# Five loads of each preparation, and the stores behind the scan, issued from GpSimd's queue instead of SyncE's

## The chip, the cores and the metric

The kernel runs on one core of one Trainium2 chip. The metric is the device time of one execution in microseconds, as the median of several runs. TensorE does the matrix products, VectorE (DVE in the profile) and ScalarE (ACT) the elementwise work. SyncE (SP) and GpSimd (POOL) issue the DMAs; GpSimd also runs a few memsets. Each engine works through its own instructions in order, so an instruction that waits holds back whatever stands behind it on that engine, DMA issues included.

## The reference

Two groups of 512 tokens with 1024 channels go through the same two layers. Layer 0 is a bidirectional RWKV-7 mixer with 16 heads of 64 channels, layer 1 a windowed attention on an 8 x 64 grid. What matters here:

```
r, k, v = lerp(0) @ w_r, lerp(1) @ w_k, lerp(2) @ w_v ;  z = xn @ w_z
kk = k * k_k ;  kk = kk / max(sqrt(sum(kk * kk)), 1e-12)          # per head
for d in range(2):                                                # forward and backward
    decay = exp(-exp(w_log(w0[d] + tanh(xw @ w1[d]) @ w2[d])))
    a     = sigmoid(a0[d] + (xa @ a1[d]) @ a2[d])
    k_d   = k * (1 + (a - 1) * k_a)
    y    += scan: S_t = S_{t-1} (diag(decay_t) - kk_t (kk_t a_t)^T) + v_t k_d_t^T ;  y_t = S_t r_t
x = x + rms(out(y) * silu(z)) ;  q, k, v, z = rms(x) @ w_in + b_in
o = softmax(q k^T / 8 + bias, in a window) v ;  y = x + rms((o * silu(z)) @ w_ao + b_ao)
```

All arithmetic is float32. A large product is done as three passes on values split into a high and a low part.

## The kernel before

A tile is 128 partitions by 512 columns of float32, 256 KB. The work has three parts.

**The part before the scan** loads the two inputs, normalizes them and makes z and k of the first group. Its stores go through SyncE, because the attribute `away` is False.

**The scan** (`scan_phase`) is woven from threads. The scan is done in 64 steps: eight chunks of 64 tokens, for each of two groups and four pairs of channel groups. Beside it run the large products of the layer: r and v of group 0, then k, r, v and z of group 1, then the first output projection and part of the second layer's input projection. Their weights come in through `raw` buffers (three of them), are split into `whi` and `wlo`, and multiplied at lines 811 to 813; their operands come in through `xr`.

Before the steps of a pair can run, two preparations (`prep`, one per channel group of 128 channels, 16 in all) have to be done. A preparation begins with five loads: the reciprocal norms `rb` in two halves, `k`, the low-rank factors `w2`, and `r`. Its first arithmetic is line 863 on DVE, which needs `k` and `rb`; line 865 on ACT and line 867 on DVE split `w2`; the products with `r` come later, at line 925. The tiles `rb`, `k` and `r` have one buffer each, so that the next preparation's loads wait until the one before has read them: `rb` until line 928 of its second direction, `k` until line 940, `r` until line 976. The tile for `w2` is one of the five `tmp` buffers. A preparation makes, for each direction, a 1 MB tile `ab` that goes to DRAM (line 944), from where the steps fetch it (`cab`), and at the end the tile `ks` (line 976), which is saved as well.

**The part behind the scan** (`rest`) finishes the input projections of the second layer, runs the attention heads beside them, and ends with the output projection of the second group. The projections are saved to DRAM (q, k, v, z), and `heads` loads them again.

What sets the order of the work: in the scan the order of TensorE, DVE and ACT is written out by a planner that works while the kernel is built. It keeps a clock per engine and per DMA issuer, and steps the thread of the best rank whose inputs will be there. A DMA on SyncE moves that issuer's clock by 380 ns, a DMA on GpSimd by 900 ns (`Clock.one`); its landing follows from the same formula for both. The order within SyncE's and GpSimd's own queues, and all orders before and behind the scan, are made by the scheduler of the framework, which has a timeline of its own. All orders are fixed before the kernel runs.

DMA issuers: `load` always uses SyncE. `save` asks `store(kind)`, which is GpSimd while `away` is True and the kind is none of y, x1 and h. `scan_phase` sets `away` to True at its start, `rest` to False. Stores on GpSimd's queue in the scan are thus `ab`, `ks`, r, v and its transposed form `vt`, k and z of group 1, and the first q, k, v, z of layer 1. At the start of the scan GpSimd also clears two large `MT` tiles (line 1659), and in every direction of a preparation it sets a pad of the tile `e` (line 902).

Of the kernel before, what the change touches and what calls it, by code (L numbers as in the profile page):

```python
# [19 lines left out]
P = 128  # L20
T = 512
# [210 lines left out]
class Trunk:  # L232
# [96 lines left out]
    def store(self, kind):  # L329
        return self.nc.gpsimd if self.away and kind not in ("y", "x1", "h") else self.nc.sync  # L330

    def load(self, dst, src):
        self.nc.sync.dma_start(dst, src)
        return dst

    def vectors(self):
# [495 lines left out]
    def prep(self, s, p):  # L832

        nc, sp = self.nc, self.sp
        vt, gps, act = nc.vector, nc.gpsimd, nc.scalar
        c3 = lambda t: t.rearrange("p (c t) -> p c t", c=NCH)
        half = lambda h: slice(64 * h, 64 * h + 64)
# [15 lines left out]
                yield "S"  # L853
        k, r, rb = b("k"), b("r"), b("rb")
        for h in range(2):
            self.load(rb[half(h)], sp["rn", s, 0][2 * p + h:2 * p + h + 1, :].to_broadcast([64, T]))
        self.load(k, sp["k", s, p])
        w2l, w2h = b("w2l", (P, 4 * P), 1, F32R), b("w2h", (P, 4 * P), 1, F32R)
        w2 = self.load(self.tmp(), self.a["lora2"][p])
        self.load(r, sp["r", s, p])  # L860
        yield "D", None, need(k, rb)
        kk = rb
        vt.scalar_tensor_tensor(kk, k, self.vec("kk", p), rb, op0=ALU.mult, op1=ALU.mult)
# [10 lines left out]
        for d in range(2):  # L874
            ths = []
            for q, bias in ((d, 8 * d + p), (2 + d, 16 + 8 * d + p)):
                yield "P", free, lambda c: max(room(c), need(w2l, w2h)(c))
                ps = self.p("pm")
                h = self.hid[q]
# [605 lines left out]
    def out1(self, s):  # L1485
        nc = self.nc
        x = self.os[s]
        acc = self.t("acc1", pool=self.ap)
        hs = []
        for p in range(NP):  # L1490
            ps = yield from self.gemm(self.weight(self.a["w_ao"][p]), x, self.OUT1[p % 4])
            h = self.t("oa", (P, T), NP, F32, self.ap)
            nc.scalar.activation(h, ps, AF.Identity, bias=self.vec("bo", p))
            self.sumsq(acc, h, p, nc.vector if p == NP - 1 else nc.vector)
            hs.append(h)
            yield
        yield from self.rstds(acc, lambda: self.mm)
        rstd = acc
        for k, h in enumerate(hs):
            x = self.load(self.t("xr", bufs=self.NXR), self.sp["x1", s, k])  # L1500
            one = nc.vector.scalar_tensor_tensor(h, h, self.vec("post1", k), rstd, op0=ALU.mult, op1=ALU.mult)
            self.behind(one, self.mq)
            (nc.vector if k % 2 else nc.vector).tensor_tensor(h, h, x, op=ALU.add)
            nc.sync.dma_start(self.a["y"][s][k * P:(k + 1) * P, :], h)
            yield

    def by_token(self):
# [211 lines left out]
    def run(self):  # L1719
        self.todo = [(s, pb) for s in range(2) for pb in range(4)]  # L1720
        self.made, self.hid, self.shift = set(), {}, {}
        self.did = Counter()
        self.xz, self.os = [], [[], []]
        self.spare = None
        self.away = False
        mid, prep, first = ExitStack(), ExitStack(), ExitStack()
        self.banks(mid, pf=1, pm=5 - self.SG - self.ZY, us=1)
        if self.SG:
            self.banks(mid, pg=self.SG)
        self.zs = ExitStack()  # L1730
        self.banks(self.zs, zy=self.ZY)
        self.gt = "zy"
        self.lp = self.pool(first, "right")
        a = self.prelude(0)
        for _ in range(self.FIRST):
            next(a)
        a = both(a, self.prelude(1))
        run(self.columns(0, "z", self.xz), (a, 1))
        run(self.columns(0, "k", self.shifted(0, 1)), (a, 1))
        run(a)  # L1740
        self.xr = self.shifted(0, 0)
        first.close()
        self.front = self.pool(mid, "right")
        self.pp = self.pool(prep, "right")
        self.AHEAD, self.AHEADW = self.SCAN_A, self.SCAN_W
        self.scan_phase(mid)
        self.rest(prep, mid)

    def rest(self, prep, mid):
        self.away = False  # L1750
        prep.close()
        mid.close()
        self.banks(self.stack, pg=self.PG, pt=self.PT, po=1, sc=1, pm=5 - self.PG - self.PT)
        self.gt = "pg"
        self.ap = self.pool(self.stack)
        queue = [self.heads(0, p) for p in range(self.NPA)]

        def attention():
            while True:
                if queue and next(queue[0], self) is self:  # L1760
                    queue.pop(0)
                    continue
                yield

        a = attention()
        for p in range(self.NPA, NP):
            run(self.inproj(0, self.xa, p), (a, self.POST0))
            queue.append(self.heads(0, p))
        run(self.out0(1), (a, self.POST))
        while queue:  # L1770
            next(a)
        o = self.out1(0)
        if self.HS:
            with self.tc.high_priority(self.HS):
                next(o)
        n = KT * NP
        for _ in self.norm0(1):
            for _ in range(min(n, 3)):
                next(o)
                n -= 1  # L1780
        for _ in range(n):
            next(o)
        x = self.x1
        xt = self.by_token()
        for p, cs in [(p, range(4)) for p in range(6)] + [(6, range(3)), (7, range(3)), (6, (3,)), (7, (3,))]:
            run(self.inproj(1, x, p, cs), (a, self.POST3), (o, self.POST2), (xt, self.POST4))
            if 0 in cs:
                queue.append(self.heads(1, p))
        run(o)
        while queue:  # L1790
            next(a)
        self.last()
# [125 lines left out]
```

## Time and profile before

| | |
|---|---|
| median of 3 runs | 1663.77 us (1659.5 to 1666.94) |
| the profiled execution: its own time | 1661.37 us |
| its span, first to last instruction | 1659.6 us |
| mean granted TensorE clock in it | 0.979 |
| scan, about | 170 to 1165 us of the span |
| DMAs issued in the scan, SyncE and GpSimd | 678 and 183 |
| DMAs issued behind the scan, SyncE and GpSimd | 312 and 1 |

In a row of a timeline the columns are start, duration, engine, line, operation, tiles, count, and in brackets the idle time of the engine before it and what ended it. "SPq" is SyncE issuing a DMA. In a row of the waits the columns are who waited for what, the time in total, how many times, and the longest. In a table by windows each engine has its busy time and the number of its instructions, then come the granted clock, the busy share of the DMA engines and the rate.

### The profile page before, as it was taken

The page shows a single profiled execution, that of the slowest core. Times are in us where ns is not written, and L with a number is a line of the kernel's source. Part 1 is how long each engine was busy: PE and PEld are TensorE (multiplying, and loading weights), DVE is VectorE, ACT ScalarE, POOL GpSimd, SP SyncE. Part 2 cuts the span into 40 slices and gives each one's busy share as a digit, 9 for nine tenths or more (in the row PEclk, how much of TensorE's full clock was granted, in tenths as well). Part 3 has the DMA queues.
Part 4 walks back from the last instruction along what each step waited for, and adds up shares of the span by engine and source line. Part 5 has one row for each costly group of instructions (what it writes and reads, how often), then busy time and mean ns, then how long its engine had stood idle before and what let it go on. Part 6 is the DMA issues. An engine that isn't in the chain of part 4 may idle for free.

```text
span 1659.6 us, 46414 instructions
## 1 busy us (share of the span) xinstructions
PE 1557.8 (94%) x18826; PEld 1193.4 (72%) x18826; DVE 1226.3 (74%) x2725; ACT 984.7 (59%) x1979; POOL 145.4 (9%) x278
## 2 busy tenths in 40 slices
PE   7989888898989998999988999999999999999998
PEld 5867566776767776776766777777777788777776
DVE  8995669688789787897788897855676585754564
ACT  5443665766756677665575665454677665555562
POOL 0000113311101224010000011000000000000000
PEclk9989999999999999999987999999999999999999
DMA  6435678776676788675867675554864346655553
GB/s 212 160 126 173 206 243 280 221 244 214 228 255 225 222 260 247 219 255 173 253 220 228 196 253 165 182 189 129 289 219 156 102 153 229 214 159 172 165 159 108
DMA packets 179894, 336.27 MB, mean 203 GB/s; under 512 B 20928, under 2 KB 53824, under 8 KB 179680
## 3 DMA queue, kind: packets, MB, share of 16 engines
q1 hardware_dynamic: 160864, 268.28, 50.2%
q0 software_dynamic: 18816, 65.02, 11.9%
q8 instruction: 148, 2.42, 0.6%
q14 instruction: 66, 0.54, 0.1%
HBM read 227.71 MB, written 105.51 MB: 201 GB/s over the span
## 4 chain that ended last, share of the span: by engine, by line
PE 46%; DVE 7%; DMA 6%; ACT 5%; issue 3%; POOL 0%; SPq 0%; DVEq 0%; ACTq 0%; POOLq 0%
PE pg L428 6%; PE pg L429 5%; PE pg L430 5%; PE pm L811 4%; PE pm L812 3%; PE pm L813 3%; PE sc L1437 2%; PE pf L1099 2%; DMA dk<-tmp 2%; PE po L1470 2%; PE us L1218 1%; PE pt L1455 1%; PE zy L1171 1%; PE us L1198 1%; PE zy L1222 1%
## 5 line engine op out<-in xcount | busy, mean ns | idle before, releaser
L811 PE MATMUL pm<-act,whi 128*128 128x512 f32 x640 | 283.6, 443 | 11.9 <-ACT whi L730 5.0
L812 PE MATMUL pm<-act,whi 128*128 128x512 f32 x640 | 257.1, 402 | 10.6 <-DVE act L758 6.5
L813 PE MATMUL pm<-act,wlo 128*128 128x512 f32 x640 | 256.1, 400 | 6.0 <-DVE wlo L732 5.9
L811 PEld LDWEIGHTS pm<-act,whi 128*128 128x128 f32 x640 | 122.0, 191 | 55.3 <-issue 11.4
L377 ACT CAST whi<-raw 128x512 fp32r<-128x512 f32 x148 | 91.5, 618 | 114.0 <-PE pg L429 67.1
L428 PE MATMUL pg<-act,whi 128*128 128x512 f32 x384 | 157.9, 411 | 0.4 <-DVE tmp L1393 0.4
L430 PE MATMUL pg<-act,wlo 128*128 128x512 f32 x384 | 152.1, 396 | 0.0
L429 PE MATMUL pg<-act,whi 128*128 128x512 f32 x384 | 152.0, 396 | 0.0
L812 PEld LDWEIGHTS pm<-act,whi 128*128 128x128 f32 x640 | 122.5, 191 | 36.6 <-DVE act L758 15.8
L813 PEld LDWEIGHTS pm<-act,wlo 128*128 128x128 f32 x640 | 122.4, 191 | 36.2 <-DVE wlo L732 9.6
L378 DVE TENSOR_TENSOR wlo<-raw,whi 128x512 fp32r<-128x512 f32 x148 | 101.5, 687 | 54.6 <-ACT whi L377 52.6
L732 DVE TENSOR_TENSOR wlo<-raw,whi 128x512 fp32r<-128x512 f32 x160 | 109.0, 684 | 35.5 <-ACT whi L730 35.2
L730 ACT CAST whi<-raw 128x512 fp32r<-128x512 f32 x160 | 97.9, 618 | 44.6 <-PE pm L812 23.4
L428 PEld LDWEIGHTS pg<-act,whi 128*128 128x128 f32 x384 | 72.2, 188 | 15.8 <-issue 3.3
L430 PEld LDWEIGHTS pg<-act,wlo 128*128 128x128 f32 x384 | 72.2, 188 | 15.5 <-issue 0.7
L429 PEld LDWEIGHTS pg<-act,whi 128*128 128x128 f32 x384 | 72.4, 189 | 13.2 <-issue 1.5
L1003 DVE TENSOR_TENSOR etmp<-N 128x30 f32<-128x30 f32 (+14 forms) x240 | 78.6, 328 | 4.3
L1005 DVE TENSOR_TENSOR N<-etmp,N 128x30 f32<-128x30 f32 (+14 forms) x240 | 78.7, 328 | 4.0
L1448 DVE CUSTOM_DVE_ANT_0 sb<-sc,bias 128x256 f32<-128x256 f32 x128 | 49.3, 419 | 34.6 <-PE pt L1455 22.7
L1451 ACT ACTIVATE sb<-sb,mx 128x256 f32<-128x256 f32 x128 | 64.0, 503 | 8.6 <-DVE mx L1450 8.1
L1099 PE MATMUL pf<-cab 64*64 64x128 f32 (+1 forms) x2048 | 66.6, 266 | 0.8 <-issue 0.8
L1210 ACT COPY X<-us 64x256 f32<-64x256 f32 x128 | 46.9, 366 | 25.3 <-PE zy L1077 21.4
(401 smaller groups left out, 3603.0 us busy)
## 6 DMA issues: line engine op xcount, KB each, us to landing
dab<-ab POOLq DMA_DIRECT2D x32, 1024.0 KB, 7.0
cab<-dab SPq DMA_DIRECT2D x64, 512.0 KB
raw<-in_w_in_dram SPq DMA_DIRECT2D x128, 256.0 KB
bias<-in_rpb_dram SPq DMA_DIRECT2D x32, 384.0 KB
raw<-in_w_z_dram SPq DMA_DIRECT2D x32, 256.0 KB
raw<-in_w_k_dram SPq DMA_DIRECT2D x32, 256.0 KB
raw<-in_w_r_dram SPq DMA_DIRECT2D x32, 256.0 KB
k<-dk SPq DMA_DIRECT2D x32, 256.0 KB
```

The lines of the kernel that those rows point to most:

```text
L377: self.nc.scalar.copy(hi, src)
L378: (eng or self.nc.vector).tensor_tensor(lo, src, hi.bitcast(F32), op=ALU.subtract)
L428: nc.tensor.matmul(ps, hi, x[k][0], start=(k == 0), stop=False)
L429: nc.tensor.matmul(ps, hi, x[k][1], start=False, stop=False)
L430: self.mm = nc.tensor.matmul(ps, lo, x[k][0], start=False, stop=(k == KT - 1))
L730: nc.scalar.copy(hi, raw[h])
L732: nc.vector.tensor_tensor(lo, raw.pop(h), hi.bitcast(F32), op=ALU.subtract)
L811: nc.tensor.matmul(ps, hi[:, at], xh, start=(k == 0), stop=False)
L812: nc.tensor.matmul(ps, hi[:, at], xl, start=False, stop=False)
L813: nc.tensor.matmul(ps, lo[:, at], xh, start=False, stop=(k == KT - 1))
L1005: vt.tensor_tensor(N[:, q + 1:, :q], tv, N[:, q + 1:, :q], op=ALU.add)
L1099: end = nc.tensor.matmul(st.f[half(a), h, 0, d, g] if st.last else st.f[half(a), h, :, d, g], ab[half(h), d, g, 2 * e[d] + 1 - a], rt if s ...
```

## The change

`load` gets a flag that sends a DMA to GpSimd's queue, and the five loads of a preparation set it: 16 x 5 = 80 DMAs in the scan. Behind the scan `away` stays True, so that the saves of q, k, v and z (10 each) and of `xt` (8, in `by_token`) go through GpSimd's queue; so do the 8 stores of the first group's output in `out1`. That makes 56 more. The stores of kinds y, x1 and h, and the last output's in `last`, stay on SyncE. The planner's rule for a DMA on GpSimd now applies to the 80 loads.

```diff
-    def load(self, dst, src):
-        self.nc.sync.dma_start(dst, src)
+    def load(self, dst, src, far=False):
+        (self.nc.gpsimd if far else self.nc.sync).dma_start(dst, src)
         return dst
...
         for h in range(2):
-            self.load(rb[half(h)], sp["rn", s, 0][2 * p + h:2 * p + h + 1, :].to_broadcast([64, T]))
-        self.load(k, sp["k", s, p])
+            self.load(rb[half(h)], sp["rn", s, 0][2 * p + h:2 * p + h + 1, :].to_broadcast([64, T]), True)
+        self.load(k, sp["k", s, p], True)
         w2l, w2h = b("w2l", (P, 4 * P), 1, F32R), b("w2h", (P, 4 * P), 1, F32R)
-        w2 = self.load(self.tmp(), self.a["lora2"][p])
-        self.load(r, sp["r", s, p])
+        w2 = self.load(self.tmp(), self.a["lora2"][p], True)
+        self.load(r, sp["r", s, p], True)
...
-            nc.sync.dma_start(self.a["y"][s][k * P:(k + 1) * P, :], h)
+            nc.gpsimd.dma_start(self.a["y"][s][k * P:(k + 1) * P, :], h)
...
     def rest(self, prep, mid):
-        self.away = False
         prep.close()
```

## The prediction

> **What bounds the kernel now.** I read the page's line of busy times first, then the table by windows.
>
> ```profile
> PE 1557.8 (94%) x18826; PEld 1193.4 (72%) x18826; DVE 1226.3 (74%) x2725; ACT 984.7 (59%) x1979; POOL 145.4 (9%) x278
> ...
> 170.00:420.00 250.00, 224.46 (x2921) 168.26 (x2922) 190.48 (x359) 163.74 (x326) 54.02 (x87) 0.97 0.73 236
> 420.00:560.00 140.00, 131.58 (x2354) 97.06 (x2356) 109.77 (x207) 92.25 (x178) 16.22 (x28) 1.00 0.72 233
> 560.00:1000.00 440.00, 406.06 (x7149) 309.20 (x7138) 368.47 (x717) 284.83 (x553) 60.84 (x100) 0.96 0.72 230
> 1000.00:1165.00 165.00, 162.94 (x3058) 124.71 (x3057) 110.84 (x222) 80.36 (x150) 11.88 (x19) 1.00 0.52 163
> 1165.00:1440.00 275.00, 269.74 (x1603) 215.21 (x1602) 185.50 (x594) 176.32 (x394) 0.54 (x1) 1.00 0.59 194
> 1440.00:1660.00 220.00, 209.86 (x1144) 163.12 (x1142) 122.76 (x371) 106.76 (x244) 0.00 (x0) 0.99 0.50 156
> ```
>
> TensorE sets the time: a change pays or costs only as far as TensorE's idle time changes. That is 25.5, 8.4, 33.9 and 2.1 us in the four windows of the scan (70.0 us together) and 5.3 and 10.1 us in the two behind it. No relief of a queue can win more than that. In the scan's 995 us DVE idles 215.4 us (995 less its four busy times), ACT 373.8 us.
>
> How much of it is owed to DMAs, the view of waits, cut to the scan and then to what lies behind, tells:
>
> ```profile
> ACT whi L730 <- DMA raw<-in_w_v_dram: 7.7, 2, 4.9
> ACT whi L730 <- DMA raw<-in_w_r_dram: 6.0, 3, 3.3
> ACT act L756 <- DMA xr<-dlz: 4.3, 1, 4.3
> DVE rb L863 <- DMA k<-dk: 2.1, 1, 2.1
> ACT w2h L865 <- DMA tmp<-in_lora_dram: 1.5, 1, 1.5
> ...
> PE sc L1437 <- DMA k<-dk: 2.1, 4, 0.6
> PEld sc L1437 <- DMA k<-dk: 2.0, 2, 1.1
> ```
>
> The first five rows are the waits of the scan that either name a moved load or a load that shares SyncE's queue with it: 21.6 us, all on DVE and ACT, which have 589.2 us of idle time between them. So DMA is not what DVE and ACT mostly wait for, and the gain to be had is small from the start.
>
> **The change, part by part.**
>
> **A, the first preparation.** It is the one place where the moved loads meet a long instruction on their new engine:
>
> ```profile
> 183.84 0.58 SPq L333 DMA_DIRECT2D k<-dk  x1
> ...
> 185.39 3.56 POOL L1659 MEMSET MT<- 128x2048 f32 x2 [29.58 <-DMA raw<-in_w_r_dram]
> ...
> 189.00 0.75 DVE L863 SCALAR_TENSOR_TENSOR rb<-k,cv,rb 128x512 f32<-128x512 f32 x1 [2.06 <-DMA k<-dk]
> 192.62 0.69 DVE L732 TENSOR_TENSOR wlo<-raw,whi 128x512 fp32r<-128x512 f32 x1 [0.35 <-ACT whi L730]
> ...
> L327 POOL DMA_DIRECT2D dr<-tmp x16: 540/541/673, 188.9 to 538.5; - x16
> ...
> DMA to landing us min/median/max: 2.3/4.4/8.7
> ```
>
> GpSimd waits 29.58 us at the two memsets and is through them at 185.39 + 3.56 = 188.95. If the loads stand behind them, the two halves of `rb` take 2 x 0.54 (a 256 KB DMA on GpSimd occupies it for 540 to 673 ns; I use the least for a half), `k` goes out at 190.0 and lands 2.3 to 4.4 us later (least and median of GpSimd's 256 KB stores, the nearest rows for a load on that queue): 192.3 to 194.4 instead of 189.0, so 3.3 to 5.4 us late. Behind line 863 on DVE stands the weight split at 192.62, which feeds the large products. The planner's clock does not count these memsets, as its count is reset behind them. If the scheduler puts the loads ahead of them the cost is 0. I take 3 us, with 0 and 5.4 as ends.
>
> **B, the other 15 preparations.** On GpSimd's queue the loads stand behind the `ks` store of the preparation before, which waits for line 976. The tightest case, and a usual one:
>
> ```profile
> 211.41 0.33 SPq L333 DMA_DIRECT2D k<-dk  x1
> ...
> 214.39 0.55 POOL L327 DMA_DIRECT2D dks<-kp  x1 [0.89 <-DVE kp L976]
> 217.65 0.54 POOL L327 DMA_DIRECT2D dr<-tmp  x1 [2.71 <-ACT tmp L642]
> ...
> 219.12 0.75 DVE L863 SCALAR_TENSOR_TENSOR rb<-k,cv,rb 128x512 f32<-128x512 f32 x1
> ...
> 615.41 0.57 POOL L327 DMA_DIRECT2D dks<-kp  x1
> ...
> 627.84 0.74 DVE L863 SCALAR_TENSOR_TENSOR rb<-k,cv,rb 128x512 f32<-128x512 f32 x1
> ```
>
> In the second preparation `k` would go out at 214.94 + 2 x 0.54 = 216.0 and land at 218.3 to 220.4, between 0.8 us early and 1.3 us late for 219.12. In the tenth, from 615.98 on, it lands at 619.4 to 621.5, more than 6 us ahead of 627.84. I set B at 0; the cover is the distance between a preparation's end and the next one's first read, and if it is gone every late microsecond stalls DVE. The issue itself costs nothing: 80 x 0.54 = 43 us more on an engine that is busy for 145.4 us.
>
> **C, what queues behind the waiting loads.** The buffer waits of the moved loads leave SyncE's queue and enter GpSimd's:
>
> ```profile
> SPq L333 <- DVE pp L928: 15.8, 10, 4.6
> SPq L333 <- DVE kp L976: 6.6, 7, 1.7
> SPq L333 <- DVE th L940: 6.2, 8, 2.9
> ```
>
> These 28.6 us hold up the stores of r, v and `vt` there; ACT, which needs the stored tiles' buffers back, would be late next. At TensorE's share of DVE's idle time, 70.0 / 215.4 = 0.33, the upper end is 9.3 us; the lower is 0, where the stores go out in the gaps they now wait in. I take 0, since GpSimd idles nine tenths of the time.
>
> **D, SyncE's queue without the 80 loads.** What the backlog costs now shows at the tenth preparation, in SyncE's timeline and then in the chain of waits:
>
> ```profile
> 609.24 0.32 SPq L333 DMA_DIRECT2D k<-dk  x1
> 612.64 1.34 SPq L333 DMA_DIRECT2D tmp<-in_lora_dram  x1
> ...
> 628.50 0.32 SPq L333 DMA_DIRECT2D sz<-dz  x1
> ...
> 616.84 8.13 DMA raw<-in_w_v_dram
> 628.92 3.76 DMA raw<-in_w_z_dram
> 855.12 6.57 DMA xr<-dlz
> ```
>
> A weight load of 256 KB took 8.13 us to land after two of the moved loads, each of the same size, in the 8 us before it; the next in the chain, with one load of that size just ahead, took 3.76 us. With them on the other queue it should land some 4 us sooner. But the bytes are the same, and DMA engines are busy 0.72 of these windows, so part of it stays. TensorE's share of such waits, 70.0 / 589.2 of 21.6 us, is 2.6 us, which I take; ends 0 and -11 (8.13 and 6.57 each shortened to 3.76, that is 4.4 + 2.8, and the 2.1 and 1.5 us of the moved loads, all felt in full: 10.8).
>
> The Trainium skill, DMA: Bandwidth & Descriptors, section Issuing engines are not separate DMA queues, says that DMAs from any issuer end on the same 16 DMA engines, and issuing from several saves only the time to initiate them. By it D and E are nothing, and the sum ends 4.1 us higher, still inside the forecast's own range. The 8.13 against 3.76 us does not settle it, as either load may have waited for bandwidth.
>
> **E, the stores behind the scan.** SyncE's timeline, and in the chain of waits a store and the load of the same tile behind it (the chain has four such places, and this is one):
>
> ```profile
> 1434.62 0.90 SPq L333 DMA_DIRECT2D bias<-in_rpb_dram  x2
> ...
> 1435.61 6.10 DMA dk<-tmp
> 1441.73 2.67 DMA k<-dk
> ```
>
> The store waits behind 768 KB of bias tables. On GpSimd's queue the same store took 4.4 us at the median, so `k` comes back about 2 us sooner. TensorE's idle time at these products is 2.1 + 2.0 = 4.1 us in all (the two rows of sc above), of which I take 1.5 as won. The ends are -4.1, if all of it goes, and +2.6: GpSimd's slowest store took 8.7 us, 2.6 more than the 6.10 here, and if that held at all four places with a quarter of it felt (TensorE idles 10.1 us of the last window, DVE 97.2, so a quarter is generous), it is 4 x 2.6 / 4. The 8 stores of the output and the q, v, z and `xt` stores are read later or not at all; what covers them is TensorE's work in the last two windows.
>
> **F, a new order.** The planner prices a load on GpSimd at 900 ns of its queue's clock and one on SyncE at 380, so from the first preparation on it may step other threads first, and TensorE, DVE and ACT get another order throughout the scan. Nothing in the trace prices that. The nearest rows are the windows with products and preparations: idle shares of 25.5 / 250, 8.4 / 140 and 33.9 / 440, so 10.2%, 6.0% and 7.7%. An order as good as the best of them over 830 us would idle 49.9 us, as bad as the worst 84.8 us, against 67.9 us now: -18 to +17. I take 0.
>
> **The sum**: 3 + 0 + 0 - 2.6 - 1.5 + 0 = -1.1 us, on 1661.37 us of the profiled execution: 1660.3. That execution lies 2.4 us under the median of 1663.77, so the forecast against the median is 1662.7, no change.
>
> **Rivals.**
>
> **Held loads, slower.** The place is GpSimd's queue ahead of the five loads. It is in order, and the waits that stand in it are long:
>
> ```profile
> POOL e L902 <- DVE ab L925: 192.6, 22, 39.8
> POOL dk L327 <- ACT tmp L642: 43.7, 5, 19.0
> ```
>
> If the loads land behind one store more that waits for ACT, as the one at 217.65 above, `k` goes out at 218.19 + 1.08 = 219.3 and lands at 221.6 to 223.7: 2.5 to 4.6 us late. Were that so at all 16 preparations, 3.5 us on DVE each at 0.33 are 18 us: 1682. It decides as soon as the wait ahead of the loads is longer than the lead that B gives, about 1 us at the second preparation and 6 at the tenth. Against it: most of the long waits end with GpSimd having nothing else to do.
>
> **Relief felt in full, faster.** D at its end of -10.8 and E at -4.1, with A at 3: -12, 1652. For it: the chain of waits runs through these DMAs. Against it: a chain has neighbours that are nearly as late.
>
> **The loads change nothing because they are hidden anyway** is the forecast itself; that the change does not do what it says can be excluded, as a queue is named by the engine that issues.
>
> **How the numbers follow.** No change is what this kernel's measurement can't tell from zero, 0.5% or 8.3 us. The forecast has 0.38, with a range of its own of 1655 to 1672. Held loads, or an order on the bad side of F, have 0.34: F's positive end and A, B and C all point there. Relief or a lucky order has 0.28. The range runs from 1645 (F's lower end) to 1686 (the slower rival and a little of F).
>
> **What would show it.** For A: line 863's first run at 192 to 194 us. For B: no DVE wait for `k` at the other preparations. For D: the waits of ACT for `raw` and `xr` shrink from 18.0 us. For E: the store in the chain at 4 to 5 us, not 6. For F: another count of products in the same windows. I would be wrong if TensorE's idle time in the scan left 50 to 85 us, or if the windows behind the scan, which I expect within 2 us of before, changed by more.

## The result and the profile after

| | before | after |
|---|---|---|
| median, 4 runs each | 1661.63 us | 1691.47 us (1687.10 to 1695.23) |
| ratio to before, 95% interval | | 1.0163 [1.0139, 1.0187] |
| the profiled execution: its own time | 1661.37 us | 1687.10 us |
| its span | 1659.6 us | 1685.3 us |

The change makes the kernel slower by 1.63%, 27 us, and the time lies above the top of the predicted range. The page's line of busy times and the table by windows of the changed kernel follow. The first three windows have the times of those of before, though not quite the same work; the others end at the same stages, some 25 us later:

```profile
PE 1561.3 (93%) x18806; PEld 1193.1 (71%) x18806; DVE 1225.3 (73%) x2725; ACT 986.8 (59%) x1979; POOL 219.9 (13%) x414
```

```profile
170.00:420.00 250.00, 209.53 (x2725) 157.56 (x2723) 175.50 (x334) 151.62 (x298) 67.49 (x111) 0.94 0.69 219
420.00:560.00 140.00, 131.17 (x2161) 96.41 (x2161) 109.80 (x206) 89.77 (x176) 24.98 (x45) 0.98 0.69 225
560.00:1000.00 440.00, 399.57 (x7286) 300.44 (x7291) 359.29 (x701) 287.14 (x558) 79.33 (x134) 0.97 0.70 224
1000.00:1190.00 190.00, 185.71 (x3275) 142.37 (x3275) 131.95 (x259) 92.97 (x174) 15.33 (x25) 1.00 0.56 180
1190.00:1465.00 275.00, 269.28 (x1570) 213.02 (x1569) 184.27 (x590) 174.94 (x392) 17.39 (x32) 0.99 0.59 191
1465.00:1686.00 221.00, 212.66 (x1182) 166.67 (x1180) 124.64 (x377) 108.75 (x247) 13.56 (x25) 0.99 0.51 160
```

TensorE, DVE and ACT are busy for as long as before, to within 4 us. What grew is TensorE's idle time in the scan: 40.5 + 8.8 + 40.4 + 4.3 = 94.0 us, against 70.0 before. These 24 us are nearly all of the 25.7 us by which the two spans differ. Behind the scan TensorE idles 5.7 + 8.3 = 14.0 us, against 15.4. So the loss sits in the scan, most of it in its first 250 us (40.5 against 25.5), and nothing was lost or won back behind it that matters. The prediction had named this sign of being wrong: TensorE's idle time in the scan left 50 to 85 us.

The view of waits of the changed kernel, cut to the scan, only the rows that end with a DMA (who waited for what, us in total, times, longest):

```profile
ACT whi L730 <- DMA raw<-in_w_v_dram: 13.5, 3, 6.3
DVE ab L925 <- DMA dab<-ab: 8.6, 3, 3.9
DVE rb L863 <- DMA k<-dk: 6.7, 1, 6.7
ACT w2h L865 <- DMA tmp<-in_lora_dram: 4.5, 3, 3.2
ACT act L756 <- DMA xr<-dlv: 3.1, 3, 1.3
...
ACT whi L730 <- DMA raw<-in_w_z_dram: 3.0, 1, 3.0
...
ACT whi L730 <- DMA raw<-in_w_o_dram: 2.6, 1, 2.6
ACT whi L730 <- DMA raw<-in_w_in_dram: 2.4, 1, 2.4
ACT whi L730 <- DMA raw<-in_w_k_dram: 1.4, 1, 1.4
```

The weights and operands that stayed on SyncE, and should have come sooner, are waited for longer: 13.5 + 3.1 + 3.0 + 2.6 + 2.4 + 1.4 = 26.0 us. Before, the rows of this kind were 18.5 us, the 18.0 of the prediction and a row of 0.5. DVE waits for `k` only once in 16 preparations.

That once is the first preparation, in the timeline of GpSimd and then of DVE:

```profile
183.74 3.56 POOL L1659 MEMSET MT<- 128x2048 f32 x2 [29.06 <-DMA raw<-in_w_r_dram]
187.24 1.18 POOL L333 DMA_DIRECT2D rb<-drn  x2
188.42 0.56 POOL L333 DMA_DIRECT2D k<-dk  x1
...
192.22 0.75 DVE L863 SCALAR_TENSOR_TENSOR rb<-k,cv,rb 128x512 f32<-128x512 f32 x1 [6.73 <-DMA k<-dk]
```

The loads stand behind the two memsets, and line 863 starts at 192.22.

### The profile page after: what moved, and what is told of

The parts are those of the page before. It is cut to its first block, busy times and chain, and to the rows that moved or that the text cites. A ratio compares the mean times of both kernels' runs of the same rounds, so it can differ in the third digit from the quotient of the medians.

```text
span 1685.3 us, 46459 instructions
## 1 busy us (share of the span) xinstructions
PE 1561.3 (93%) x18806; PEld 1193.1 (71%) x18806; DVE 1225.3 (73%) x2725; ACT 986.8 (59%) x1979; POOL 219.9 (13%) x414
## 4 chain that ended last, share of the span: by engine, by line
PE 62%; DVE 12%; DMA 10%; ACT 9%; issue 6%; POOL 1%; SPq 0%; DVEq 0%; ACTq 0%; POOLq 0%
PE pg L428 6%; PE pg L429 6%; PE pg L430 6%; PE pm L811 5%; PE pm L812 4%; PE pm L813 4%; PE pf L1099 2%; PE us L1218 2%; PE sc L1437 2%; PE po L1470 2%; PE zy L1171 2%; PE pt L1455 2%; PE zy L428 2%; PE us L1198 2%; PE zy L1222 2%
## 5 line engine op out<-in xcount | busy, mean ns | idle before, releaser
L811 PEld LDWEIGHTS pm<-act,whi 128*128 128x128 f32 x640 | 122.4, 191 | 53.6 <-issue 13.5
```

Of the source, the lines that this page charges most:

```text
L811: nc.tensor.matmul(ps, hi[:, at], xh, start=(k == 0), stop=False)
```

## The experiments

The trace leaves two causes that the change brings together. **The order theory**: the planner prices a load on GpSimd at 900 ns instead of 380, and so writes another order for TensorE, DVE and ACT; that order is worse. **The queue theory**: GpSimd's queue delivers the loads later, or holds back stores. The planner's price and the issuing engine can be separated, since the planner only reads a clock per issuer; the third part, the stores behind the scan, can be separated as well.

**The three parts alone, and the loads once with each order.** `loads_only` is the change without its stores, `stores_only` the change without its loads. The other two give the 80 loads an issuer and a planner's clock that don't belong together:

```diff
 # both: Clock.note looks the clock up by the name of the loaded tile
-            end = max(end, self.one(e, i))
+            end = max(end, self.one(self.priced.get(i.outs[0].bass_ap.tensor.name, e) if type(i).__name__ == "InstDMACopy" else e, i))
 # loads_old_order: GpSimd issues, the planner prices them as on SyncE
+        (self.nc.gpsimd if far else self.nc.sync).dma_start(dst, src)
+        return self.clock.priced.update({dst.tensor.name: "S"} if far else {}) or dst
 # order_only: SyncE issues, the planner prices them as on GpSimd
+        self.nc.sync.dma_start(dst, src)
+        return self.clock.priced.update({dst.tensor.name: "G"} if far else {}) or dst
```

> Only the 80 loads of the preparations are on GpSimd's queue; everything behind the scan is as before. The theory of the new order and the theory of the loads on GpSimd's queue both expect nearly all of the loss here, 1.014 to 1.018 of before; a theory that the stores behind the scan cost the time expects 1.000.

> Only the 56 stores behind the scan are on GpSimd's queue. The order theory and the queue theory of the loads both expect 0.998 to 1.002 of before: in the changed kernel the lag is about 26 us at the scan's end and about 26 us at the end of the run. A theory that the stores cost the time expects 1.010 or more.

> The 80 loads are on GpSimd's queue, but the planner prices them as SyncE's, so that TensorE, DVE and ACT keep the order of before to the last instruction. Order theory: 0.998 to 1.004 of before, as only the loads' lateness is left. Queue theory: 1.013 to 1.018, the whole loss, as the loads and the transfers beside them are as late as in the changed kernel.

> The 80 loads stay on SyncE's queue, but the planner prices them as GpSimd's, so that TensorE, DVE and ACT have in the scan the order of the changed kernel. Order theory: 1.012 to 1.018 of before, the whole loss. Queue theory: 0.997 to 1.003.

Measured, as ratios to before with 95% intervals:

| the 80 loads | order of before | order by the price of 900 |
|---|---|---|
| on SyncE | 1 | `order_only` 1.0095 [1.0073, 1.0117] |
| on GpSimd | `loads_old_order` 1.0040 [1.0025, 1.0054] | `loads_only` 1.0175 [1.0154, 1.0196] |

`stores_only` gave 0.9987 [0.9971, 1.0004]. So the stores behind the scan cost nothing that can be measured, and both theories hold a part: the new order alone costs 0.95% of 1662 us, 15.8 us, with not one load moved; the queue alone, with the order of TensorE, DVE and ACT as it was, costs 0.40%, 6.6 us. `order_only` met neither of its two expected ranges. Its changed order includes that within the queues of SyncE and GpSimd, which is made anew with it. Together the two parts cost 1.75%, 29.1 us, so some 6.7 us more than added up; the three intervals together leave 1 to 12 us for this.

The table by windows, one row for the scan, first of `order_only`, then of `loads_old_order`:

```profile
170.00:1180.00 1010.00, 920.87 (x15394) 696.08 (x15395) 771.52 (x1492) 618.02 (x1200) 142.51 (x232) 0.96 0.66 216
```

```profile
170.00:1180.00 1010.00, 933.07 (x15483) 707.07 (x15484) 782.62 (x1507) 623.45 (x1209) 186.94 (x314) 0.97 0.67 218
```

TensorE idles 89.1 us in `order_only` and 76.9 us in `loads_old_order`, 19 and 7 us more than the 70.0 of before. Their spans are 22.4 and 7.7 us longer (the profiled execution of `order_only`, 1683.76 us, is the slowest of its five, whose median is 1678.51). Both losses are idle TensorE in the scan, as in the whole change.

What a worse order looks like is seen at one place of `order_only`, in the chain of waits, then in the timelines of SyncE, GpSimd and ACT:

```profile
270.98 7.52 DMA dab<-ab
...
286.74 10.18 DMA raw<-in_w_v_dram
...
286.74 1.74 SPq L333 DMA_DIRECT2D raw<-in_w_v_dram  x1
...
283.64 0.90 POOL L944 DMA_DIRECT2D dab<-ab  x1
...
297.02 0.62 ACT L730 CAST whi<-raw 128x512 fp32r<-128x512 f32 x1 [8.14 <-DMA raw<-in_w_v_dram]
```

The same stretch before, in the timelines of GpSimd, SyncE and ACT:

```profile
282.40 0.89 POOL L944 DMA_DIRECT2D dab<-ab  x1
...
279.78 0.33 SPq L333 DMA_DIRECT2D raw<-in_w_v_dram  x1
...
285.88 1.20 SPq L333 DMA_DIRECT2D raw<-in_w_v_dram  x1
...
291.06 0.62 ACT L730 CAST whi<-raw 128x512 fp32r<-128x512 f32 x1 [2.51 <-PE pm L812]
...
309.44 0.65 ACT L730 CAST whi<-raw 128x512 fp32r<-128x512 f32 x1
```

In both kernels a weight load of 256 KB goes out at nearly the same time, some 3 us behind a 1 MB store of `ab`, and in both it lands late. The chain gives it 10.18 us in the new order. In the trace of before, the last of the events that tell of this load's end stands at 295.44, 9.56 us after its issue. What differs is when the load is needed. Before, the cast at 291.06 reads the load of 279.78, which had landed by 282.90; the one at 309.44 is the cast that waits for the semaphore of the load of 285.88, 23.6 us after its issue, so nothing stands still. In the new order ACT is ready for its load at 288.88, 2.1 us after the issue, and stands for 8.14 us. The rows of the windows over these 15 us, `order_only` and then before:

```profile
285.00:300.00 15.00, 6.93 (x63) 5.74 (x65) 8.88 (x24) 3.62 (x7) 5.50 (x9) 0.77 0.93 272
```

```profile
285.00:300.00 15.00, 14.43 (x134) 11.87 (x134) 14.25 (x31) 5.21 (x10) 3.44 (x6) 0.89 0.86 289
```

TensorE is busy for 6.93 us of them instead of 14.43, while the DMA engines are busier, 0.93 against 0.86, and move no more. So at this place the new order asks for a weight too soon, and the transfer is hardly later than before. Nor do the weight loads land later on average: worked out from the same events in the traces, the 162 weight loads of the scan took 4.41 us from issue to landing before and 4.31 us in `order_only`. The changed kernel has such a place a little later: its chain of waits shows a load of the same matrix with 10.38 us.

```profile
289.88 10.38 DMA raw<-in_w_v_dram
```

The queue's own part is seen in `loads_old_order`, whose order of the three engines is that of before. Its waits in the scan, and then line 863's first run in the timeline of DVE:

```profile
DVE ab L925 <- DMA dab<-ab: 7.1, 4, 2.3
DVE rb L863 <- DMA k<-dk: 6.5, 1, 6.5
ACT whi L730 <- DMA raw<-in_w_v_dram: 6.1, 2, 4.6
ACT act L756 <- DMA xr<-dlz: 5.2, 1, 5.2
ACT w2h L865 <- DMA tmp<-in_lora_dram: 4.6, 3, 3.2
ACT whi L730 <- DMA raw<-in_w_r_dram: 4.5, 3, 1.9
ACT whi L730 <- DMA raw<-in_w_o_dram: 3.1, 1, 3.1
...
192.80 0.75 DVE L863 SCALAR_TENSOR_TENSOR rb<-k,cv,rb 128x512 f32<-128x512 f32 x1 [6.48 <-DMA k<-dk]
```

There is no relief for the loads left on SyncE. These rows have 6.1 + 5.2 + 4.5 + 3.1 = 18.9 us of ACT's waits for `raw` and `xr`, and with one of 0.8 that is not shown 19.7, against 18.5 before. Such a sum varies: in `stores_only` and in a second run of that kernel (below), whose scan has the order and the issuers of before, it is 10.9 and 19.1 us. The landings are steadier. The weight loads of the scan land 4.33 us after their issue on average here, 4.41 us before, and after 4.27 and 4.40 us in those two runs. And the load that took 8.13 us at the tenth preparation before takes some 6.8 us here, in the timelines of SyncE and ACT, though no moved load stands ahead of it on SyncE any more:

```profile
621.48 0.33 SPq L333 DMA_DIRECT2D raw<-in_w_v_dram  x1
...
628.31 0.62 ACT L730 CAST whi<-raw 128x512 fp32r<-128x512 f32 x1 [1.55 <-DMA raw<-in_w_v_dram]
```

Three waits grew. That for `k` at the first preparation went from 2.1 to 6.5 us. That for `w2` went from 1.5 to 4.6, of which 3.2 are at the first preparation too, in ACT's timeline:

```profile
193.66 0.62 ACT L865 CAST w2h<-tmp 128x512 fp32r<-128x512 f32 x1 [3.24 <-DMA tmp<-in_lora_dram]
```

And that for the stores of `ab`, which now share their queue with the loads, went from 5.0 (a row of the same view of before, below; 5.5 and 5.6 in the two runs with moved stores) to 7.1.

```profile
DVE ab L925 <- DMA dab<-ab: 5.0, 4, 2.2
```

For the stores the chain of waits between 1425 and 1600 us, shares by line, before and then in `stores_only`:

```profile
by line: PE pg L428 18.9%; PE pg L429 18.5%; PE pg L430 18.1%; DMA dk<-tmp 15.5%; PE sc L1437 9.1%; DMA k<-dk 6.1%; PE po L1470 4.7%; PE pt L1455 4.5%; PE pm L1424 2.7%; SPq L333 1.1%; issue 0.5%; DVE tmp L1393 0.4%; SPq L327 0.0%
```

```profile
by line: PE pg L428 25.5%; PE pg L429 25.0%; PE pg L430 24.4%; PE sc L1437 7.7%; PE po L1470 7.0%; PE pt L1455 6.7%; PE pm L1424 2.8%; PE pg L1558 0.4%; PE pg L1557 0.4%; PE pg L1559 0.3%
```

The store and the load of `k`, 21.6% of that stretch of the chain before, are gone from it, and the chain is all TensorE. What that is worth is small: the ratio gives 2.2 us won, with an interval from 4.8 us won to 0.7 us lost, so TensorE was nearly as late. The order of the engines behind the scan is another one too in `stores_only`, so that the two are not told apart.

**Is it the price of 900, or any other order?** The loads stay on SyncE in four kernels; only the price and the planner's clock for them differ. The number is put into the planner, on SyncE's clock (S) or on GpSimd's (G); the lines shown are those for 600 ns on GpSimd's clock:

```diff
-    def one(self, e, i):
+    def one(self, e, i, far=0):
...
-                self.t[e] = issued = max(issued, self.t["P"]) + 900.0
+                self.t[e] = issued = max(issued, self.t["P"]) + (far or 900.0)
...
-            end = max(end, self.one(e, i))
+            far = type(i).__name__ == "InstDMACopy" and i.outs[0].bass_ap.tensor.name in self.priced; end = max(end, self.one("G" if far else e, i, 600.0 if far else 0))
```

> All DMAs as before, on SyncE. The planner prices the 80 loads on SyncE's clock at 360 instead of 380 ns, a change that means nothing physically, but about a third of TensorE's instructions in the scan's order change place. If any redrawn order is worse, as the order of before is a favourable one among many, 1.004 to 1.012 of before; if it is GpSimd's price that makes the order worse, 0.998 to 1.002.

> All DMAs on SyncE; the 80 loads are priced at 900 ns on SyncE's clock. If the high price, by which the planner expects the loads later than they come, makes the order worse: 1.008 to 1.015, the same as with 900 ns on GpSimd's clock. If any redrawn order is worse: 1.003 to 1.015, without a pattern in the price.

> All DMAs on SyncE; the 80 loads are priced at 380 ns on GpSimd's clock. If the 900 ns are to blame: 0.998 to 1.003. If any redrawn order is worse: 1.003 to 1.015.

> All DMAs on SyncE; the 80 loads are priced at 600 ns on GpSimd's clock. If the loss grows with the price: between the runs with 380 and with 900 ns on this clock, about 1.004. If any redrawn order is worse: anywhere from 1.003 to 1.015.

And two prices close to 900, which should be as bad if the height matters and anywhere if each order is a draw by itself:

> All DMAs on SyncE; the 80 loads priced at 880 ns on GpSimd's clock, nearly the price of the changed kernel, yet another order. If a price of this height makes any order bad: 1.007 to 1.012 of before, as with 900. If the order drawn at 900 is an unlucky one among redrawn orders: 1.002 to 1.005, as in the other four draws.

> The same with 920 ns. If the height of the price is to blame: 1.007 to 1.013. If 900 is an unlucky draw: 1.002 to 1.005.

| price, clock | ratio |
|---|---|
| 360, SyncE's | 1.0024 [0.9999, 1.0048] |
| 380, GpSimd's | 1.0032 [1.0011, 1.0053] |
| 600, GpSimd's | 1.0035 [1.0015, 1.0055] |
| 900, SyncE's | 1.0032 [1.0015, 1.0049] |
| 880, GpSimd's | 1.0081 [1.0050, 1.0111] |
| 900, GpSimd's (`order_only`) | 1.0095 [1.0073, 1.0117] |
| 920, GpSimd's | 1.0075 [1.0052, 1.0098] |

No redrawn order is better than that of before, and even a price that differs by 20 ns costs about 0.2%, though that one's interval reaches 1. The four that are not near 900 on GpSimd's clock lie close to the lower end of what was expected if any redrawn order is worse (1.003, or 1.004 for 360), one of them below it, so they decide little. The three near 900 on GpSimd's clock, three orders that differ from each other, are the worst, as expected if the height of the price matters; so their loss is not the bad luck of one draw. But the same 900 on SyncE's clock is as cheap as 600.

**The first preparation.** As `loads_old_order`, but its five loads stay on SyncE:

```diff
-        self.load(k, sp["k", s, p], True)
+        self.load(k, sp["k", s, p], s + p > 0)
```

(and so for `rb`, `w2` and `r`.)

> As the run with the loads on GpSimd's queue in the order of before, but the first preparation's five loads stay on SyncE, so that they don't stand behind the two memsets. If the first preparation is a part of what the queue costs: 2 to 3.5 us less than that run, 1.002 of before, and line 863's first run back at 189 us. If all of the queue's cost comes from later places: 1.004.

Measured: 1.0023 [1.0004, 1.0041]. Line 863's first run in its timeline of DVE is back where it was before:

```profile
188.15 0.75 DVE L863 SCALAR_TENSOR_TENSOR rb<-k,cv,rb 128x512 f32<-128x512 f32 x1 [2.42 <-DMA k<-dk]
```

The difference to `loads_old_order` is 0.17%, 2.8 us; the two intervals overlap, so the size isn't proven, but it is the size that the start of line 863 gives.

**The stores once more**, in 12 executions after the 11 of `stores_only`, as 2 us would make them worth keeping:

> The kernel with only the stores behind the scan on GpSimd's queue again, with more rounds. If faster stores spare the products at line 1437 their wait for k: 0.998 to 0.999 of before, 2 to 4 us. If the redrawn order behind the scan gives that back: 1.000.

Measured: 0.9988 [0.9962, 1.0014]. The median is 1658.12 us against 1660.48. It agrees with `stores_only`, and is still not to be told from no change.

**What makes 900 on GpSimd's clock bad.** One guess was that the planner, with loads and stores on one clock, believes that queue to be full and lets the stores come late. Here the loads get 900 or 880 on a clock of their own (one line of the kernel, written here on three):

```diff
+            own, self.own = (self.t["G"], self.own) if far else (0, self.own); self.t["G"] = self.own if far else self.t["G"]
             end = max(end, self.one("G" if far else e, i, 900.0 if far else 0))
+            self.own, self.t["G"] = (self.t["G"], own) if far else (self.own, self.t["G"])
```

> All DMAs on SyncE; the 80 loads are priced at 900 ns, but on a clock of their own, so that they don't push the planned times of GpSimd's stores back, nor the stores theirs. If the loss of the orders at 880 to 920 comes from loads and stores sharing one planned queue: 1.002 to 1.005 of before. If it comes from the 900 ns by themselves: 1.007 to 1.010.

> The same with 880 ns, a second draw. Shared queue: 1.002 to 1.005. The price by itself: 1.007 to 1.010.

Measured: 1.0057 [1.0036, 1.0077] and 1.0087 [1.0057, 1.0117]. The second is as bad as with the shared clock at 880; the first lies between the two expectations, below the 1.0095 at 900, with intervals that touch. So sharing the clock is not shown to be the cause, and a part of it is not excluded.

**Does a better price save the moved loads?** GpSimd issues one of them in some 550 ns, as the group of these issues in the changed kernel shows (least, median and most; from when to when):

```profile
L333 POOL DMA_DIRECT2D rb<-drn x32: 528/534/654, 187.2 to 963.9; - x32
L333 POOL DMA_DIRECT2D k<-dk x16: 544/562/585, 188.4 to 969.1; - x16
```

So a price of 600 is nearer to the truth than 900. `loads_G600` is `price_G600` with the loads on GpSimd:

> The 80 loads really on GpSimd's queue, with the order that the price of 600 ns gives. If order and queue add up: 1.0035 + 0.004, so 1.006 to 1.009 of before, half the loss of the changed loads. If the queue's cost depends on the order, as the 0.4% in the order of before and 0.8% in that at 900 suggest: up to 1.012.

Measured: 1.0093 [1.0066, 1.0120]. It is better than `loads_only` with its 1.0175, but worse than `price_G600` with the loads on SyncE, at 1.0035. In this order the move itself costs 1.0093 / 1.0035, 0.58%; in the order of before it cost 0.40%, in that of 900, 1.0175 / 1.0095, 0.79%. With intervals of about 0.2% on each part these three can't be told apart for certain. None is a gain.

No version beats before by more than can be measured; the best is the one with the moved stores alone.

## Why the prediction was wrong

**The step that failed is F**, the new order. Its mechanism was named, and its bounds were drawn from the idle shares of three windows as -18 to +17 us; the step then took the middle, 0, without a reason for it. `order_only` measures it by itself at +15.8 us, close to the upper end. To take the middle is to assume that a redrawn order is as often better as worse. Nine redrawn orders with the loads on SyncE lie between +0.24% and +0.95%, none below 0, though the interval of one reaches it. The order of before is at the good end of those the planner makes here, so the term should have been set above 0; how far, no row of the trace before could tell. F's sign in the table was as foretold: the first window has 2725 products instead of 2921, and it is the order's, as `order_only` has 2726 there and `loads_old_order` 2915.

**The range failed by adding.** Its top, 1686, held the slower rival and a little of F, not F's end as well. The runs had both: 15.8 for the order, 6.6 for the queue, and 6.7 that only the two together cost, less some 2 for the stores: 27.

**A was right.** Line 863 started at 192.22 where 192 to 194 was foretold, and undoing it gave 2.8 us for the 3 taken, a size that the intervals do not prove. That `w2` is late there too, by 3.2 us, the step had not said.

**B was right.** At the other 15 preparations DVE has no wait for `k`, and in the old order ACT waits 0.7 us for `w2` at two of them, 1.4 together, where it had waited 1.5 us at one before.

**C was too low at 0**, though inside its bounds. Stores of `ab` that share the queue are waited for 7.1 us instead of 5.0 in the old order. The step looked at r, v and `vt` only and left out `ab`, which the scan's own work at line 925 waits for. At the share of 0.33 that the prediction used, that comes to 2.1 x 0.33 = 0.7 us.

**D was wrong.** It took 2.6 us as won. In the old order the waits for `raw` and `xr` are 19.7 us, not fewer than 18.5, and the weight loads land after 4.33 us on average instead of 4.41. The weight load at the tenth preparation still takes some 6.8 us with the moved loads off its queue, so most of its 8.13 us was not the price of the loads ahead of it on SyncE. The rule weighed there (the Trainium skill, DMA: Bandwidth & Descriptors, section Issuing engines are not separate DMA queues), that other issuers save no more than time to initiate, agrees with these numbers. A's 2.8 and the 0.7 above leave some 3 us of the queue's 6.6 unassigned. The step's sum of 21.6 us had also left out rows of 2.3 and 0.5 us for other loads on SyncE, which at its share are 0.3 us.

**E was right in its mechanism**: the store's way through the chain vanished, and the stores of `k` landed after 4.9 us at the median in `stores_only`, where 4 to 5 was foretold. Its 1.5 us agree with the 2.2 and 2.0 us of two runs, whose intervals both include 0, so the gain itself is not shown. The windows behind the scan stayed within 2 us, as foretold.

**The rivals.** The 0.34 for held loads or an order on the bad side of F covers what happened, by the order. Held loads by itself was on the right side, but not by its mechanism: `k` was late at one preparation, not at 16, and the queue alone cost 6.6 us, not 18. Relief felt in full is refuted by D.

**What stays open**: why prices near 900 on GpSimd's clock, or on one of their own, make worse orders than the same price on SyncE's clock, and why the order's and the queue's costs add up to more than their sum. That the new order asks for a weight before it can have landed, as at 286 us above, is shown at that place. That such places make up the whole 15.8 us is not: ACT's waits for `raw` and `xr` are 29.2 us in `order_only`, against 10.9 to 19.1 in the three kernels whose scan is that of before, but no run takes them away.

## What to carry to other kernels

Where a planner with prices writes the order, moving an instruction to another engine changes the order of everything, and this can cost more than the move: here 15.8 us against 6.6. Price the new order as a term of its own, with a mean above 0 where, as here, the present order is the only one that has been measured, and separate it on the chip by giving the planner one issuer and the kernel another. A load put on another queue comes behind what that queue already holds, here two memsets that made `k` some 3 us late. The loads on the queue it left need not land sooner: here 4.33 us after their issue, against 4.41.

## What had not been expected

A change of 20 ns in the planner's price of 80 loads, 380 to 360, with not one instruction moved to another engine, gave 1.0024 [0.9999, 1.0048], some 4 us, which is as much as A and E together. And a weight load of 256 KB took 10.18 us to land in one order and 9.56 us in the other, issued within 1 us of the same moment and some 3 us behind a 1 MB store in both. Only the order that needed it at once stood still.
